# Expert routing by top-8 search with indices on two token halves, in a two-layer encoder

## The chip, the cores and the metric

One core of one Trainium2 chip runs the whole program. The metric is the device time of one execution in microseconds (us). The core has TensorE (PE; PEld is its weight load), VectorE (DVE), ScalarE (ACT), GpSimd (POOL) and SyncE (SP), each with its own queue of instructions in order; 16 DMA engines are shared by the queues that issue DMAs (here SP, ACT and POOL).

## The reference, cut to what matters

Two layers, 512 tokens of width 1024, each with a mixer, a cross-attention and a mixture of 16 experts, in which every expert picks its 64 best tokens:

```python
def expert_choice_moe(h, w_router, w_gate, w_up, w_down):   # h: (1, 512, 1024), normed x
    cap = EC_CAPACITY_FACTOR * S // N_EXPERTS                # 64
    affinity = jax.nn.softmax((h @ w_router).astype(jnp.float32), axis=-1)
    gate, idx = lax.top_k(jnp.swapaxes(affinity, 1, 2), cap)
    x_in = jax.vmap(lambda hb, ib: hb[ib])(h, idx)
    a = jnp.einsum('becd,edf->becf', x_in, w_gate)
    u = jnp.einsum('becd,edf->becf', x_in, w_up)
    y = jnp.einsum('becf,efd->becd', jax.nn.silu(a) * u, w_down)
    y = y * gate[..., None].astype(y.dtype)
    return ...                                               # y added at rows idx
```

## The kernel before, in words

The tokens stand on the 128 partitions in four blocks (b). A layer runs the mixer, the cross-attention and the experts in this order. The last stage of the cross-attention adds its output to x (out_block), transposes x (features), makes router logits (logits, scaled) and the softmax (affinity, `aff`), and turns it to 16 experts by 512 tokens (turned, into `pT`). out_block also writes the plain x of each block to `xrows` in HBM, from ScalarE's queue (L876).

**Routing (L943 to L991).** Eight rounds on VectorE take the eight largest of each expert's row (MAX8, L976) and replace them by -1 (L977). Where the row is below -0.5 the token is chosen (L981); a scan over the tokens numbers the chosen ones (L982), transposes bring mask and numbers back to tokens on partitions (L987), and `pos` holds the place of each token in each expert's list, or 0 (L991). `warm` puts idle matmuls on TensorE behind some of these steps. GpSimd meanwhile splits affinity and norm factor into high and low parts (`affs`, with the token number beside them). In layer 0 the matmuls of next_keys, for layer 1, fill TensorE at this time, and ScalarE copies their result to kT (L854).

**Experts (L993 to L1224).** They run in eight pairs, one expert's 64 tokens in each half of the array's columns. one_hot compares `pos` with the numbers 1 to 64 on VectorE. fetch multiplies the one-hots with `affs` (four matmuls, L1089), casts the token number (L1091), gathers the 128 rows from `xrows` by an indirect DMA on GpSimd's queue (L1093) and adds the two parts of gate and norm factor. features_of transposes the rows (L1072) and scales them (L1075). up_half (L1108) and down (L1127) are the expert matmuls; selection transposes the one-hots (L1081) and copies them on ScalarE (L1083), and scatter multiplies them with y and adds to x (L1141, L1142). Iteration e does pair e's gate and up projections and pair e-1's down projection and scatter; pair e+2's fetch stands at its end.

**The weights** (512 KB tiles `ew`, 192 per layer) come through a ring of buffers on SP's queue (L1028). Some lie in memory that the stage before frees (`ewb`, EW_B of them); a tile loads when its buffer's last reader is done. `lnf`, the gain of the last norm, is loaded from ScalarE's queue (L1215) into a buffer of the tag "oh".

**The order.** The program is written once, and a planner puts each engine's instructions in order at build time, from its own costs, with earlier program text first among what it believes ready. It can move work far ahead of its text, and its order holds whatever the real times are. Buffers of a tag are handed on in turn, and a DMA issue can wait for a DMA that it shares no data with, as a weight load on SP does for that of `lnf`. The lines that set the ring and the warming:

```python
        ring = [(ew, "ew", EW_KEEP)] * EW_KEEP + [(kt, "kt", 1)] * (l > 0) + [(ewa, "ew", EW_A)] * (EW_A - pre)
        once = {22: (mp, "y", 2), 23: (mp, "y", 2)}
        early = len(ring)
        ring += [(ewb, "ew", EW_B)] * EW_B + [(ewa, "ew", EW_A)] * pre
```

Of the kernel before, what the change touches and what calls it, by code (L numbers as in the profile page):

```python
# [16 lines left out]
P = 128  # L17
D = 1024
# [10 lines left out]
EW_B = 12  # L29
# [4 lines left out]
WARM_T = (1, 3)  # L34
# [23 lines left out]
def kernel(ctx: ExitStack, tc: tile.TileContext, a: dict, out: bass.AP):  # L58
# [31 lines left out]
    iota = const.tile([P, CAP], F32, name="iota")  # L90
    ids = const.tile([P, NB], F32, name="ids")
    fold = const.tile([P, NE], F32, name="fold")
    ident_r = const.tile([P, P], F32R, name="ident_r")

    def late_constants():
        nc.sync.dma_start(iota, a["iota"])
        nc.sync.dma_start(ids, a["ids"])
        nc.sync.dma_start(fold, a["fold"])
        nc.vector.tensor_copy(ident_r, ident)
# [108 lines left out]
    for l in range(L):  # L208
# [657 lines left out]
        aff = const.tile([P, NB, NE], F32, tag="aff", name=nm("aff"))  # L866
# [39 lines left out]
        def affinity(b):  # L906
# [37 lines left out]
        small = mp.tile([P, 1024], F32, tag="xg", name=nm("small"), bufs=3)  # L944
        affr = small[:, 0:2 * NB * NE].rearrange("p (b e c) -> p b e c", b=NB, e=NE)
        mkt = small[:, 256:256 + NB * NE].rearrange("p (g b e) -> p g b e", g=4, b=NB)
        m8 = small[:NE, 512:512 + CAP]

        affs = mp.tile([P, NB, NE // 2, 10], F32R, name=nm("affs"))
        pos = mp.tile([P, 4, NB, 4], F32, name=nm("pos"))  # L950
# [4 lines left out]
        parts = affs.rearrange("p b q c -> p (b q) c")[:, :, 0:8].rearrange("p q (i h c) -> p q i h c", i=2, h=2)  # L955
        whole = affr.rearrange("p b (q i) c -> p (b q) i c", i=2)
        nc.gpsimd.tensor_copy(parts[:, :, :, 0, :], whole)
        nc.gpsimd.tensor_tensor(out=parts[:, :, :, 1, :], in0=whole, in1=parts[:, :, :, 0, :].bitcast(F32),
                                op=ALU.subtract)
        for q in range(NE // 2):  # L960
            nc.gpsimd.tensor_copy(affs[:, :, q, 8:10], ids.unsqueeze(2).broadcast_to([P, NB, 2]))
        if l < L - 1:
            next_keys(range(NK0, ND))
        work = mp.tile([P, 2, S], F32, tag="oh", name=nm("work"), bufs=2)
        wk, cs = work[:NE, 0, :], work[:NE, 1, :]
# [24 lines left out]
        nc.scalar.copy(mkt, pv[0])  # L990
        nc.vector.tensor_tensor(out=pos, in0=pv[1], in1=mkt, op=ALU.mult)  # L991
# [58 lines left out]
        ohs = {}  # L1050

        def one_hot(g):

            oh = mp.tile([P, NB, 256], F32R, tag="oh", name=nm("oh"), bufs=2)
            for b0, nb in ([(b, 1) for b in range(NB)] if g == 0 else [(0, NB)]):
                nc.vector.tensor_tensor(
                    out=oh[:, b0:b0 + nb].rearrange("p b (e s) -> p (b e) s", s=CAP),
                    in0=pos[:, g, b0:b0 + nb].rearrange("p b e -> p (b e)").unsqueeze(2).broadcast_to([P, nb * 4, CAP]),
# [244 lines left out]
```

## Time and profile before

| what | us |
|---|---|
| median of 3 runs (lowest, highest) | 1205.39 (1204.15, 1206.23) |
| the profiled execution's own time | 1205.65 |
| its span, first to last instruction | 1203.9 |
| TensorE busy | 1146.7 (95%) |
| VectorE busy | 622.8 (52%) |
| ScalarE busy | 500.5 (42%) |
| GpSimd busy | 197.6 (16%) |
| TensorE's share of the chain that ended last | 82% |
| the same chain over DMAs | 7% |
| the same chain over VectorE | 6% |

Busy shares are averages over stages with different limits; the chain is followed back from the last instruction to what released each step. Matmuls overlap, so the busy time of a group of matmuls is longer than the time between the starts of two groups. In the chain a line "PE ps L1108 x16" is sixteen matmul instructions; an fp32 matmul is two.

### The profile page before, as it was taken

The numbers are of one execution on the slowest core, as the hardware profiler recorded it, in microseconds if no ns is written. First come the engines' busy times: TensorE is split into PE (matmuls) and PEld (weight loads), VectorE is DVE, ScalarE is ACT, GpSimd is POOL, SyncE is SP. The second block draws the span as 40 slices with busy tenths as digits, with TensorE's granted clock in tenths as the row PEclk, the third lists the DMA queues.
The fourth block names the chain that finished last, engine by engine and source line by source line (L and its number), as shares of the span: only waits on it lengthen the run. The fifth ranks groups of instructions, "written<-read, shape, count | busy, mean of one in ns | idle before, by whom it ended". The sixth has DMA issues, their size and how long they took to land.

```text
span 1203.9 us, 16694 instructions
## 1 busy us (share of the span) xinstructions
PE 1146.7 (95%) x5992; PEld 741.2 (62%) x5992; DVE 622.8 (52%) x1405; ACT 500.5 (42%) x1140; POOL 197.6 (16%) x258
## 2 busy tenths in 40 slices
PE   7999999999997999999999999999998699999995
PEld 7977777887673444333389677778876334443332
DVE  4898877555561222222278888775465503332224
ACT  5388757464422121111154887674454021211103
POOL 2633413100011000000035333230001000000002
PEclk9999999999998999999999999999999799999998
DMA  6310011375078999999344100117813599997994
GB/s 192 129 66 19 19 36 36 123 286 221 19 286 330 415 410 416 414 411 416 156 123 132 52 19 18 36 53 261 298 35 137 214 391 416 411 414 306 349 416 179
DMA packets 78930, 260.50 MB, mean 216 GB/s; under 512 B 8704, under 2 KB 18816, under 8 KB 78848
## 3 DMA queue, kind: packets, MB, share of 16 engines
q1 hardware_dynamic: 74960, 246.23, 53.2%
q0 software_dynamic: 2304, 8.39, 1.9%
q10 hardware_dynamic: 1584, 4.83, 1.1%
q8 instruction: 47, 0.77, 0.3%
q14 instruction: 35, 0.29, 0.1%
HBM read 253.12 MB, written 6.29 MB: 215 GB/s over the span
## 4 chain that ended last, share of the span: by engine, by line
PE 82%; DMA 7%; DVE 6%; ACT 2%; issue 1%; POOL 0%; SPq 0%; POOLq 0%; DVEq 0%; ACTq 0%
PE ps L1108 17%; PE ps L147 11%; PE ps L148 10%; PE ps L149 10%; PE ps L1127 8%; PE ps L1141 5%; PE ps L410 5%; DMA ew<-moe 4%; PE ps L396 4%; DMA rows<-xrows,row 2%; PE ps L1072 2%; DVE smm L184 2%; PE ps L491 2%; PE ps L807 1%; PE ps L253 1%
## 5 line engine op out<-in xcount | busy, mean ns | idle before, releaser
L1108 PE MATMUL ps<-ew,xg 128*64 128x512 f32 x1024 | 256.6, 604 | 0.3 <-DMA ew<-moe 0.3
L1108 PEld LDWEIGHTS ps<-ew,xg 128*64 128x64 f32 x1024 | 74.6, 138 | 138.4 <-issue 121.6
L117 DVE TENSOR_TENSOR y<-ps,y 128x512 fp32r<-128x512 f32 x32 | 22.1, 692 | 216.3 <-ACT y L116 216.3
L1127 PE MATMUL ps<-ew,hT 128*64 128x512 f32 x512 | 118.5, 594 | 0.2 <-DMA ew<-moe 0.2
L117 DVE TENSOR_TENSOR wlo<-raw,whi 128x1024 fp32r<-128x1024 f32 (+2 forms) x72 | 82.0, 1143 | 56.5 <-ACT whi L116 50.5
L184 DVE TENSOR_REDUCE smm<-ps 128x1 f32<-128x512 f32 (+1 forms) x144 | 97.6, 681 | 18.2 <-PE ps L491 7.6
L190 ACT ACTIVATE P<-ps,smm 128x512 f32<-128x512 f32 x128 | 88.8, 696 | 27.8 <-DVE smm L184 22.0
L1142 DVE TENSOR_TENSOR x<-ps,x 128x512 f32<-128x512 f32 x128 | 80.7, 684 | 38.0 <-PE ps L1141 37.5
L116 ACT CAST whi<-raw 128x1024 fp32r<-128x1024 f32 (+2 forms) x72 | 70.0, 973 | 65.8 <-PE ps L148 35.9
L199 POOL TENSOR_TENSOR P<-P,smr 128x512 f32<-128x512 f32 x64 | 70.3, 1098 | 155.9 <-DVE smr L197 129.0
L116 ACT CAST y<-ps 128x512 fp32r<-128x512 f32 x32 | 18.7, 585 | 157.0 <-PE ps L1127 154.2
L1127 PEld LDWEIGHTS ps<-ew,hT 128*64 128x64 f32 x512 | 38.0, 137 | 72.9 <-issue 70.0
L396 PE MATMUL ps<-ident,P 128*128 128x128 f32 x512 | 76.9, 274 | 2.9 <-POOL P L199 0.9
L147 PE MATMUL ps<-whi,hTh 128*128 128x384 f32 (+2 forms) x224 | 79.2, 353 | 0.2 <-ACT whi L116 0.2
L148 PE MATMUL ps<-whi,hTl 128*128 128x384 f32 (+2 forms) x224 | 78.4, 350 | 0.0
L149 PE MATMUL ps<-wlo,hTh 128*128 128x384 f32 (+2 forms) x224 | 77.9, 350 | 0.0
L396 PEld LDWEIGHTS ps<-ident,P 128*128 128x128 f32 x512 | 62.6, 141 | 22.8 <-issue 4.2
L1141 PE MATMUL ps<-y,sel 128*128 128x512 f32 x256 | 70.3, 411 | 1.5 <-ACT y L116 1.5
L1093 POOL DMA_INDIRECT rows<-xrows,row x16 | 15.4, 962 | 332.0 <-DVE g L1099 296.5
L399 ACT COPY PT<-ps 128x512 f32<-128x512 f32 x96 | 56.0, 588 | 24.5 <-PE ps L396 24.0
L1141 PEld LDWEIGHTS ps<-y,sel 128*128 128x128 f32 x256 | 45.4, 188 | 31.6 <-issue 17.0
L1075 ACT ACTIVATE xg<-ps,gains 128x128 f32<-128x128 f32 x128 | 36.3, 372 | 67.7 <-PE ps L1072 67.7
(223 smaller groups left out, 2124.5 us busy)
## 6 DMA issues: line engine op xcount, KB each, us to landing
ew<-moe SPq DMA_DIRECT2D x384, 512.0 KB, 10.2
raw<-w_o SPq DMA_DIRECT2D x16, 512.0 KB, 3.8
raw<-w_mem_v SPq DMA_DIRECT2D x8, 512.0 KB, 3.4
raw<-w_mem_q SPq DMA_DIRECT2D x8, 512.0 KB, 4.5
raw<-w_mem_o SPq DMA_DIRECT2D x8, 512.0 KB, 4.1
xrows<-x ACTq DMA_DIRECT2D x8, 512.0 KB, 2.6
raw<-w_in_c SPq DMA_DIRECT2D x8, 416.0 KB, 3.6
raw<-w_in_a SPq DMA_DIRECT2D x8, 384.0 KB, 4.7
```

Source lines behind the costliest of these rows:

```text
L116: i = nc.scalar.copy(dst_hi, src)
L117: nc.vector.tensor_tensor(out=dst_lo, in0=src, in1=dst_hi.bitcast(F32), op=ALU.subtract)
L147: nc.tensor.matmul(o, lh, rh, start=start, stop=False)
L148: nc.tensor.matmul(o, ll, rh, start=False, stop=False)
L149: nc.tensor.matmul(o, lh, rl, start=False, stop=stop)
L184: nc.vector.tensor_reduce(out=m, in_=s.rearrange("p (g n) -> p g n", g=groups), axis=AX.X, op=ALU.max, negate=True)
L190: nc.scalar.activation(p[:, g * n:(g + 1) * n], s[:, g * n:(g + 1) * n], AF.Exp, bias=m[:, g:g + 1], scale=1.0 if scale is None else scale ...
L396: nc.tensor.transpose(pt[:, tb * P:(tb + 1) * P], u.p[:, tb * P:(tb + 1) * P], ident)
L1108: nc.tensor.matmul(acc[i * 64:i * 64 + 64, :], e.xg[:, k, i * 64:i * 64 + 64], ch[i][j % 2], start=k == 0, stop=k == 7)
L1127: nc.tensor.matmul(e.py[i * 64:i * 64 + 64, :], e.hT[:, f, i * 64:i * 64 + 64], ch[i][j], start=f == 0, stop=f == 3)
L1141: nc.tensor.matmul(o, sl, e.y[n][i], start=i == 0, stop=i == 1)
L1142: nc.vector.tensor_tensor(out=x[:, b, ns], in0=o, in1=x[:, b, ns], op=ALU.add)
```

## The change

Affinities are padded to 32 columns and turned so that an expert's first 256 tokens stand on one partition and its last 256 on another, 32 further on. Each round is MAX8, an index search (max_index) and a replace over 256 columns. The two sorted lists of 64 are merged by comparing the first with the reverse of the second: at each place the larger value and its token. Four small matmuls put token and gate of each pair in a column; `row`, `tok` and `gate` serve all pairs. The selection is a comparison of the token numbers 0 to 511 with `tok` on VectorE. `xrows` now holds the normed x, which ScalarE makes (rows_out) after the affinities, in halves of 256 KB; the norm factor leaves silu. Fourteen warming matmuls stand behind the first two fetches, half of the first pair's feature scaling goes to VectorE, the ring has one buffer more, `iota` is 256 KB, and `lnf` takes a buffer of the tag "rows".

```diff
-EW_B = 12
+EW_B = 13
 WARM = 3
-WARM_T = (1, 3)
+WARM_F = 14
...
-        aff = const.tile([P, NB, NE], F32, tag="aff", name=nm("aff"))
+        aff = const.tile([P, NB, 32], F32, tag="aff", name=nm("aff"))
+        nc.gpsimd.memset(aff[:, :, NE:32], 0.0)
...
             if n == 1:
-                nc.scalar.dma_start(xrows[b * P:(b + 1) * P, :], x[:, b, :])
                 ffn_norm.rstd(b)
...
         def turned(b):
             if b == 0:
                 plg["T"] = bank()
-            nc.tensor.transpose(plg["T"][:NE, b * P:(b + 1) * P], aff[:, b, :], ident)
+            h, c = 32 * (b // 2), b % 2 * P
+            nc.tensor.matmul(plg["T"][h:h + 32, c:c + P], aff[:, b, :], ident, start=True, stop=True)
+
+        def rows_out(b):
+
+            for n in range(2):
+                t = cp.tile([P, 512], F32, tag="P", name=nm("xn"), bufs=P_BUFS)
+                ns = slice(n * 512, n * 512 + 512)
+                nc.scalar.activation(t, x[:, b, ns], AF.Copy, scale=ffn_norm.r[:, b:b + 1])
+                nc.scalar.dma_start(xrows[b * P:(b + 1) * P, ns], t)
...
         turned(NB - 1)
+        for b in range(NB):
+            rows_out(b)
         pT = plg["T"]
...
+        tk = mp.tile([64, 1024], F32, tag="xg", name=nm("tk"), bufs=3)
+        wk, m8 = tk[:, 0:256], tk[:, 256:256 + CAP]
+        at8 = mp.tile([64, CAP], mybir.dt.uint32, name=nm("at8"))
+        tok = mp.tile([P, NE // 2], F32, name=nm("tok"))
+        gate = mp.tile([P, NE // 2], F32, name=nm("gate"))
+        row = mp.tile([P, NE // 2], mybir.dt.int32, name=nm("row"))
         ewb = moe.enter_context(tc.tile_pool(name=f"ewb{l}", bufs=EW_B, reuse_waits="tile"))
-        rsb = ffn_norm.r.unsqueeze(2).broadcast_to([P, NB, NE])
-        nc.gpsimd.tensor_tensor(out=affr[:, :, :, 0], in0=aff, in1=rsb, op=ALU.mult)
-        nc.gpsimd.tensor_copy(affr[:, :, :, 1], rsb)
...
         def warm(behind, n):
 
-            nc.tensor.matmul(idle[:8, 0:P], behind, ident[:NE, :], start=True, stop=True)
+            if behind is not None:
+                nc.tensor.matmul(idle[:8, 0:P], behind, ident[:64, :], start=True, stop=True)
             for _ in range(n):
                 nc.tensor.matmul(idle[:, 0:256], x[:, 0, 0:P], x[:, 0, 0:256], start=True, stop=True)
 
+
         for i in range(CAP // 8):
-            src = wk if i else pT[:NE, :]
-            nc.vector.max(out=m8[:, 8 * i:8 * i + 8], in_=src)
-            nc.vector.match_replace(out=wk, in_to_replace=m8[:, 8 * i:8 * i + 8], in_values=src, imm_value=-1.0)
+            src, best = wk if i else pT[0:64, 0:256], m8[:, 8 * i:8 * i + 8]
+            nc.vector.max(out=best, in_=src)
+            nc.vector.max_index(out=at8[:, 8 * i:8 * i + 8], in_max=best, in_values=src)
+            if i < CAP // 8 - 1:
+                nc.vector.match_replace(out=wk, in_to_replace=best, in_values=src, imm_value=-1.0)
             if i >= WARM_FROM[l]:
-                warm(m8[:, 8 * i:8 * i + 8], WARM)
-        mk = wk
-        nc.vector.tensor_scalar(mk, wk, -0.5, None, op0=ALU.is_le)
-        nc.vector.tensor_tensor_scan(out=cs, data0=ones[:NE, :].broadcast_to([NE, S]), data1=mk, initial=0.0,
-                                     op0=ALU.mult, op1=ALU.add)
-        pp = [bank() for _ in range(2)]
-        for t, src in zip(pp, (mk, cs)):
-            for b in range(NB):
-                nc.tensor.transpose(t[:, b * NE:(b + 1) * NE], src[:, b * P:(b + 1) * P], ident[:NE, :NE])
-            warm(src[:, 0:8], WARM_T[src is cs])
-        pv = [t[:, 0:NB * NE].rearrange("p (b g e) -> p g b e", g=4, e=4) for t in pp]
-        nc.scalar.copy(mkt, pv[0])
-        nc.vector.tensor_tensor(out=pos, in0=pv[1], in1=mkt, op=ALU.mult)
+                warm(best, WARM)
+
+        c = [tk[0:NE, 320 + CAP * i:320 + CAP * i + CAP] for i in range(5)]
+        m2, t1, t2, dt, later = c
+        nc.scalar.copy(m2, m8[32:32 + NE, ::-1])
+        nc.vector.tensor_copy(t1, at8[0:NE, :])
+        nc.vector.tensor_scalar(t2, at8[32:32 + NE, ::-1], float(S // 2), None, op0=ALU.add)
+        nc.vector.tensor_tensor(out=later, in0=m2, in1=m8[0:NE, :], op=ALU.is_gt)
+        nc.vector.tensor_tensor(out=dt, in0=t2, in1=t1, op=ALU.subtract)
+        nc.vector.tensor_tensor(out=dt, in0=dt, in1=later, op=ALU.mult)
+        nc.vector.tensor_tensor(out=t1, in0=t1, in1=dt, op=ALU.add)
+        nc.vector.tensor_tensor(out=m2, in0=m2, in1=m8[0:NE, :], op=ALU.max)
+
+        pk = bank()
+        for j, src in enumerate((t1, m2)):
+            for i in range(2):
+                nc.tensor.matmul(pk[i * 64:i * 64 + 64, j * 8:j * 8 + 8], src, ident[0:NE, i:NE:2], start=True, stop=True)
+        nc.vector.tensor_copy(row, pk[:, 0:8])
+        nc.scalar.copy(tok, pk[:, 0:8])
+        nc.scalar.copy(gate, pk[:, 8:16])
...
+        for p, e in enumerate(prs):
+            e.p = p
...
-                nc.scalar.activation(e.xg[:, d, :], pt[:, i * P:(i + 1) * P], AF.Copy, scale=gain(l, G_FFN, d))
+                if e.p == 0 and i % 2:
+                    nc.vector.tensor_scalar(e.xg[:, d, :], pt[:, i * P:(i + 1) * P], gain(l, G_FFN, d), None, op0=ALU.mult)
+                else:
+                    nc.scalar.activation(e.xg[:, d, :], pt[:, i * P:(i + 1) * P], AF.Copy, scale=gain(l, G_FFN, d))
 
         def selection(e):
-            pS = bank()
-            pSr = pS.bitcast(F32R)
-            for b in range(NB):
-                nc.tensor.transpose(pSr[:, b * P:(b + 1) * P], e.oh[:, b, :], ident_r)
-            e.sel = mp.tile([P, S], F32R, tag="sel", name=nm("sel"), bufs=1)
-            nc.scalar.copy(e.sel, pS)
+
+            e.sel = mp.tile([P, S], F32R, tag="sel", name=nm("sel"), bufs=2)
+            nc.vector.tensor_scalar(e.sel, iota, tok[:, e.p:e.p + 1], None, op0=ALU.is_equal)
...
         def fetch(e):
 
-            pgt = bank()
-            for b in range(NB):
-                nc.tensor.matmul(pgt[:, 0:10], e.oh[:, b, :], affs[:, b, e.p, :], start=b == 0, stop=b == NB - 1)
...
             e.rows = mp.tile([P, D], F32, tag="rows", name=nm("rows"), bufs=2)
             nc.gpsimd.indirect_dma_start(out=e.rows, out_offset=None, in_=xrows,
-                                         in_offset=bass.IndirectOffsetOnAxis(ap=at_row, axis=0))
-            e.gt = mp.tile([P, 2], F32, tag="gt", name=nm("gt"), bufs=4)
...
+                                         in_offset=bass.IndirectOffsetOnAxis(ap=row[:, e.p:e.p + 1], axis=0))
...
-        one_hot(0)
         for e in prs[:2]:
             fetch(e)
+        warm(None, WARM_F)
         for n in range(2):
             features_of(prs[0], n)
...
-            nc.scalar.activation(sg, ag, AF.Silu, scale=e.gt[:, 1:2])
-            nc.vector.scalar_tensor_tensor(out=sg, in0=au, scalar=e.gt[:, 0:1], in1=sg, op0=ALU.mult, op1=ALU.mult)
+            nc.scalar.activation(sg, ag, AF.Silu)
+            nc.vector.scalar_tensor_tensor(out=sg, in0=au, scalar=gate[:, e.p:e.p + 1], in1=sg, op0=ALU.mult,
+                                           op1=ALU.mult)
             e.hid = sg
...
-            lnf = mp.tile([P, D], F32, tag="oh", name=nm("lnf"), bufs=2)
+            lnf = mp.tile([P, D], F32, tag="rows", name=nm("lnf"), bufs=2)
             nc.scalar.dma_start(lnf, a["lnf"])
...
-    a["iota"] = np.ascontiguousarray(np.broadcast_to(np.arange(1, CAP + 1, dtype=np.float32)[None], (P, CAP)))
-    a["ids"] = np.ascontiguousarray(np.arange(S, dtype=np.float32).reshape(NB, P).T)
+    a["iota"] = np.ascontiguousarray(np.broadcast_to(np.arange(S, dtype=np.float32)[None], (P, S)))
```

## Rows read from the trace of the kernel before

**Rows 1.** Chain of waits in order of time, layer 0's experts: start us, us, what.
```profile
363.21 7.56 DMA rows<-xrows,row
...
372.84 4.75 PE ps L1108 x16
...
406.71 3.43 PE ps L1108 x16
...
453.84 6.87 PE ps L1127 x32
...
480.83 6.87 PE ps L1127 x32
...
504.44 1.86 PE ps L1108 x6
...
511.86 6.87 PE ps L1127 x32
```

**Rows 2.** Stretches of layer 1: us, busy us by engine, granted clock, DMA share, GB/s.
```profile
944.00:956.00 12.00, 7.43 (x42) 5.27 (x42) 5.05 (x17) 0.21 (x1) 2.02 (x2) 0.98 0.32 111
956.00:968.00 12.00, 10.95 (x44) 4.62 (x46) 0.00 (x0) 4.59 (x13) 0.00 (x0) 0.74 0.54 187
...
1088.00:1100.00 12.00, 12.00 (x55) 4.17 (x53) 0.00 (x0) 1.72 (x5) 0.00 (x0) 1.00 1.03 415
1100.00:1112.00 12.00, 12.00 (x49) 4.61 (x46) 3.97 (x10) 2.79 (x7) 0.94 (x1) 1.00 0.54 197
```

**Rows 3.** What SP's queue waited for: us in total, times, longest us.
```profile
SPq L1028 <- DMA lnf<-lnf: 19.5, 1, 19.5
```

**Rows 4.** The chain of waits in order of time, layer 1's experts.
```profile
952.59 4.32 DMA rows<-xrows,row
...
958.99 5.22 PE ps L1108 x16
...
1122.28 11.95 DMA ew<-moe
```

**Rows 5.** Timeline, layer 1's search: start us, us, what, idle time before it.
```profile
931.62 0.69 DVE L976 MAX8 small<-ps 16x8 f32<-16x512 f32 x1 [0.37 <-PE ps L921]
...
933.12 0.68 DVE L976 MAX8 small<-work 16x8 f32<-16x512 f32 x1
...
933.84 0.08 DVE L977 MATCH_VALUE_LOAD work<-small,work 16x8 f32 x1
933.91 0.67 DVE L977 MATCH_REPLACE8 work<-small,work 16x512 f32<-16x512 f32 x1
```

**Rows 6.** Timeline, layer 1: end of its routing, and a part of its first pair.
```profile
949.08 1.56 PE L972 MATMUL ps<-x 128*128 128x256 f32 x6
...
952.59 1.08 POOL L1093 DMA_INDIRECT rows<-xrows,row  x1 [18.87 <-DVE gt L1100]
...
972.16 0.59 PE L1089 MATMUL ps<-affs,oh 128*128 128x10 f32 x4
...
972.60 0.53 PE L1081 MATMUL ps<-ident_r,oh 128*128 128x128 f32 x4
...
973.06 7.09 PE L1108 MATMUL ps<-ew,xg 128*64 128x512 f32 x32
```

**Rows 7.** Timeline, layer 0's search and ScalarE beside its end.
```profile
345.15 0.69 DVE L976 MAX8 small<-ps 16x8 f32<-16x512 f32 x1 [0.37 <-PE ps L921]
...
355.52 1.67 ACT L854 COPY kT<-ps 128x256 f32<-128x256 f32 x4 [11.20 <-PE ps L850]
```

**Rows 8.** Groups of VectorE by shape: busy us, mean ns, idle before.
```profile
L891 DVE COPY rht<-ps 128x256 f32<-128x256 f32 x16 | 6.8, 422 | 1.4 <-ACT rht L890 0.5
...
L991 DVE TENSOR_TENSOR pos<-ps,small 128x64 f32<-128x64 f32 x2 | 0.4, 224 | 4.4 <-PE ps L987 4.4
```

**Rows 9.** Timeline, layer 0: the third pair's rows come in.
```profile
395.61 0.66 PE L1072 MATMUL ps<-ident,rows 128*128 128x128 f32 x4 [1.49 <-DMA rows<-xrows,row]
```

**Rows 10.** ScalarE's scaled copy of 128x512, group by shape.
```profile
L1160 ACT ACTIVATE ew<-ew,nr 128x512 f32<-128x512 f32 x4 | 2.9, 718 | 1.4 <-POOL nr L172 1.3
```

More of the change, by code (lines that the diff above doesn't have):

```diff
@@ L89 @@
     nc.gpsimd.memset(ones, 1.0)
-    iota = const.tile([P, CAP], F32, name="iota")
-    ids = const.tile([P, NB], F32, name="ids")
+    iota = const.tile([P, S], F32, name="iota")
     fold = const.tile([P, NE], F32, name="fold")
-    ident_r = const.tile([P, P], F32R, name="ident_r")
     def late_constants():
         nc.sync.dma_start(iota, a["iota"])
-        nc.sync.dma_start(ids, a["ids"])
         nc.sync.dma_start(fold, a["fold"])
-        nc.vector.tensor_copy(ident_r, ident)
     G_MIX, G_MEM, G_MKV, G_FFN, G_CQ, G_CKV, G_OG, G_OM = 0, 8, 16, 24, 32, 34, 35, 39
@@ L943 @@
         mp = moe.enter_context(tc.tile_pool(name=f"moe{l}", bufs=1, reuse_waits="tile"))
[L944 to L950, printed above, removed]
-        ewb = moe.enter_context(tc.tile_pool(name=f"ewb{l}", bufs=EW_B, reuse_waits="tile"))
-        rsb = ffn_norm.r.unsqueeze(2).broadcast_to([P, NB, NE])
-        nc.gpsimd.tensor_tensor(out=affr[:, :, :, 0], in0=aff, in1=rsb, op=ALU.mult)
-        nc.gpsimd.tensor_copy(affr[:, :, :, 1], rsb)
[L955 to L961, printed above, removed]
+        tk = mp.tile([64, 1024], F32, tag="xg", name=nm("tk"), bufs=3)
[4 more added lines that the diff above has]
+        row = mp.tile([P, NE // 2], mybir.dt.int32, name=nm("row"))
+        ewb = moe.enter_context(tc.tile_pool(name=f"ewb{l}", bufs=EW_B, reuse_waits="tile"))
         if l < L - 1:
             next_keys(range(NK0, ND))
-        work = mp.tile([P, 2, S], F32, tag="oh", name=nm("work"), bufs=2)
-        wk, cs = work[:NE, 0, :], work[:NE, 1, :]
         idle = bank()
         def warm(behind, n):
-            nc.tensor.matmul(idle[:8, 0:P], behind, ident[:NE, :], start=True, stop=True)
+            if behind is not None:
+                nc.tensor.matmul(idle[:8, 0:P], behind, ident[:64, :], start=True, stop=True)
             for _ in range(n):
@@ L1049 @@
         prs = [Experts() for _ in range(NE // 2)]
[L1050 to L1058, printed above, removed]
-                    in1=iota.unsqueeze(1).broadcast_to([P, nb * 4, CAP]), op=ALU.is_equal)
-            for i in range(2):
-                e = prs[2 * g + i]
-                e.p = 2 * g + i
-                e.oh = oh[:, :, i * P:i * P + P]
+        for p, e in enumerate(prs):
+            e.p = p
         def features_of(e, n):
@@ L1074, in features_of @@
                 d = n * 4 + i
-                nc.scalar.activation(e.xg[:, d, :], pt[:, i * P:(i + 1) * P], AF.Copy, scale=gain(l, G_FFN, d))
+                if e.p == 0 and i % 2:
+                    nc.vector.tensor_scalar(e.xg[:, d, :], pt[:, i * P:(i + 1) * P], gain(l, G_FFN, d), None, op0=ALU.mult)
+                else:
+                    nc.scalar.activation(e.xg[:, d, :], pt[:, i * P:(i + 1) * P], AF.Copy, scale=gain(l, G_FFN, d))
         def selection(e):
-            pS = bank()
-            pSr = pS.bitcast(F32R)
-            for b in range(NB):
-                nc.tensor.transpose(pSr[:, b * P:(b + 1) * P], e.oh[:, b, :], ident_r)
-            e.sel = mp.tile([P, S], F32R, tag="sel", name=nm("sel"), bufs=1)
-            nc.scalar.copy(e.sel, pS)
-        def fetch(e):
-            pgt = bank()
-            for b in range(NB):
-                nc.tensor.matmul(pgt[:, 0:10], e.oh[:, b, :], affs[:, b, e.p, :], start=b == 0, stop=b == NB - 1)
-            at_row = mp.tile([P, 1], mybir.dt.int32, tag="row", name=nm("row"), bufs=4)
-            nc.vector.tensor_copy(at_row, pgt[:, 8:9])
+            e.sel = mp.tile([P, S], F32R, tag="sel", name=nm("sel"), bufs=2)
+            nc.vector.tensor_scalar(e.sel, iota, tok[:, e.p:e.p + 1], None, op0=ALU.is_equal)
+        def fetch(e):
             e.rows = mp.tile([P, D], F32, tag="rows", name=nm("rows"), bufs=2)
             nc.gpsimd.indirect_dma_start(out=e.rows, out_offset=None, in_=xrows,
-                                         in_offset=bass.IndirectOffsetOnAxis(ap=at_row, axis=0))
-            e.gt = mp.tile([P, 2], F32, tag="gt", name=nm("gt"), bufs=4)
-            g2 = mp.tile([P, 2], F32, tag="g2", name=nm("g2"), bufs=2)
-            for i in range(2):
-                sl = slice(i * 64, i * 64 + 64)
-                nc.vector.tensor_copy(g2[sl, :], pgt[sl, 4 * i:4 * i + 2])
-                nc.vector.tensor_tensor(out=e.gt[sl, :], in0=pgt[sl, 4 * i + 2:4 * i + 4], in1=g2[sl, :], op=ALU.add)
+                                         in_offset=bass.IndirectOffsetOnAxis(ap=row[:, e.p:e.p + 1], axis=0))
         def up_half(e, acc, w, kc):
@@ L1177 @@
             end = e.p == NE // 2 - 1
-            if e.p % 2 == 0 and not end and e.p + 2 < NE // 2:
-                one_hot(e.p // 2 + 1)
             ag = bank()
```

4 lines of the change are left out of this document (2 added, 2 removed).

## The prediction

> **What bounds the kernel now.** I read first the page's 40 slices and its chain by engine: TensorE is busy nearly throughout and carries most of the chain, so a change that shortens VectorE's work counts only where TensorE waits for it. Then the chain in order of time, for two stretches in each layer: the routing head, between the last router logits and the first expert matmul, and the expert pairs.
>
> In the pairs the chain is TensorE after TensorE. The down projections of successive pairs start 480.83 - 453.84 = 27.0 us apart while the order is whole, and 511.86 - 480.83 = 31.0 us apart later [rows 1]. Nothing waits for weights in that 31.0: the planner has cut the matmul blocks there and put scatter pieces between. Six L1108 matmuls alone take 1.86 us, where sixteen together take 3.43, so 1.29 for six: 0.57 per break [rows 1].
>
> The weight stream is the second bound. At 415 GB/s a 524 KB tile takes 1.26 us, and a pair needs 24 tiles and a row fetch, about 31.6 us, more than a whole-order pair of TensorE. In layer 1 the stream stands partly idle while its buffers are full (DMA share 0.32 and 0.54 of a full 1.03: 8.3 and 5.7 us lost) and again at 1100 (0.54) [rows 2], where SP's queue waits 19.5 us for the load of lnf [rows 3]. Behind that the chain goes over weight tiles [rows 4]. So layer 0 is TensorE's; in layer 1's second half both bounds lie close together.
>
> **Search.** Before, from the first maximum to the first row fetch: 952.59 - 931.62 = 20.97 us in layer 1 [rows 5, 6]; 363.21 - 345.15 = 18.06 us in layer 0 [rows 1, 7]. A round is a maximum (0.68), a value load (0.08) and a replace (0.67) with 0.06 of gaps, 1.49 us, eight times [rows 5]. After, each works on 256 columns: from the groups of 256 and 64 columns one column is (422 - 224)/192 = 1.03 ns [rows 8], so 256 fewer save 0.26: 0.42 and 0.41. The trace has no index search; I price it as a load and a replace of that length (0.49 + 0.03), its nearest row. A round is 1.49 and the last, without replace, 0.97: 7 x 1.49 + 0.97 = 11.4 us against 11.9. Bounds: a free search gives 7.3; all three at full length 17.4 (a round of 2.27).
>
> The Trainium skill (Vector Engine (DVE) Microarchitecture Reference, 3.9) says that the maximum leaves no positions and that finding them is a separate value load and a streaming pass. No run here shows it; by it the free end falls away, and the sum stays.
>
> **Merge.** Removed behind the search: compare, scan, eight transposes, pos, one-hots, eight gather matmuls. Added: seven small VectorE operations at 0.22 (the 128x64 group [rows 8]) = 1.5 us, four fp32 matmuls in eight passes, two of the blocks of four that take 0.44 (972.60 - 972.16 [rows 6]) = 0.9, a cast and hand-offs, 0.5. From the first maximum to the fetch: 11.4 + 2.9 = 14.3 us. In layer 0 the reversed copy stands on ScalarE behind the kT copies, which end at 357.19, 1.3 us behind the last maximum as I place it (345.15 + 7 x 1.49 + 0.42 = 356.0) [rows 7]; VectorE has its index search and two other operations meanwhile, so I add 0.5: 14.8. Saved: 3.3 us in layer 0, 6.7 in layer 1 (the small operations at half or double: 0.8 less, 1.5 more per layer).
>
> **Rows and warming.** The first rows landed in 7.56 us in layer 0, where the stream was running [rows 1], and in 4.32 in layer 1, where it stood mostly idle [rows 2, 4]. The row writes (2 MB, 5 us of stream) now come after the norm, and one more weight tile is loaded, so layer 1's fetch falls into traffic: I take 7.0, nearer to the row with the stream running, +2.7 (bounds 0 to 3.2). The 14 warming matmuls take 14 x 1.56/3 = 7.3 us [rows 6] and fit in that landing; with rows at 4.3 they would be the last to end, so the 2.7 stands either way. They stand behind the merge's matmuls in the program, and a planner that sets them ahead costs at most that much. The granted clock was 0.74 of full in 956 to 968 [rows 2], a mixture of the levels of 1.2 and 2.4 GHz, and the first sixteen matmuls took 4.75 and 5.22 us against 3.43 [rows 1, 4]: 1.3 and 1.8 to win, 0 to lose. I take 1.0 each, since the planner may spread the warming.
>
> **Pairs.** The gather matmuls and the selection transposes hold TensorE from 972.16 to 973.06: 0.44 and 0.46 [rows 6]. Six gathers (the first two are in the head) and eight selections per layer: 2.6 + 3.7 = 6.3 us, all on the chain. What replaces them, a 128x512 compare, goes to VectorE, which waits for TensorE there; ScalarE loses its copy of the selection. With VectorE's cover gone each would cost at most a 512-column operation per pair, 0.68 by the maximum's row [rows 5]. The fetches no longer wait for TensorE: the third pair's wait of 1.49 in layer 0 [rows 9] goes. After it the next late thing is the weight stream.
>
> **What is moved.** The eight scaled copies ahead of the writes are new on ScalarE, 0.72 each [rows 10]; their issues stand on ScalarE's queue, and the later ones wait for one of five P buffers, with the affinity's exp, the merge's copy and xg behind them. I take +0.6 per layer, one copy pushed ahead of an exp (0 to two copies, 1.4). The fetch on POOL's queue now also waits for these writes; they have 14 us, and if they are late the price is one landing, up to 7.56. New weight tiles that lie over P buffers make SP's queue wait for those writes, the whole stream behind it; the idle 8.3 + 5.7 us of layer 1 [rows 2] cover that, less what the earlier start uses up. The table of 256 KB costs 0.5 us of stream at the start, beside projections: 0 (up to 0.5).
>
> **The planner's order.** Faster pairs use up the loaded tiles sooner, so the cut order may begin a pair earlier. One more cut pair costs 31.0 - 27.0 = 4.0 us [rows 1]; I take half, +2.0 per layer (from -11, no cuts, to +16, all pairs cut).
>
> **Sum.** Layer 0: -3.3 - 1.0 - 6.3 - 1.5 + 0.6 + 2.0 = -9.5. Layer 1: -6.7 + 2.7 - 1.0 - 6.3 + 0.6 + 2.0 = -8.7. The stream must allow the latter: its free run starts with the first freed buffer, 4 to 5 us earlier, one buffer more is 1.3, and the wait for lnf should shrink, since lnf now takes a rows buffer that is free earlier; I count 3 of the roughly 6 us lost in 1100 to 1112 [rows 2]. That is 8.7 too. The profiled execution took 1205.65 us (span 1203.9); less 18.2 is 1187.4. It stands 0.26 above the median of the runs, so I predict 1187.
>
> **The rivals.**
> *The stream takes layer 1's gain.* If the lnf wait stays and SP waits for the row writes, layer 1 gains 4 rather than 8.7: 1192, and up to 1200 where layer 0's stream is held too. For it: the tiles on the chain behind 1122 [rows 4]; against it: the idle 14 us.
> *The halved search is no shorter.* If operations on 64 partitions take what 512 columns take, each layer loses 6.0: 1199. For it: the halves stand on 64 partitions where 16 were, and no row shows these operations so; against it: the column slope [rows 8].
> *Slower: the order breaks up.* If the planner, with the lead used up sooner, cuts the four whole pairs of each layer as well, that is 4 x 4.0 - 2.0 = 14 more per layer, 28 in all: 1215. It decides from about 2.8 pairs per layer, where 9.1 + 2.0 are eaten. For it: the 4.0 was paid with no weight wait to justify it [rows 1]; against it: one buffer more, and about 1 us less work per pair moves the onset by less than a pair. The Trainium skill (TensorEngine Tiling (Array Packing), Key Properties) says that a change of tiling mode drains TensorE; by that rule each such cut costs, and the trace agrees with 0.57 per break [rows 1].
> *Better: the cuts vanish.* With the selection no longer on TensorE and one more buffer: 13 less in layer 0, up to 5 in layer 1: 1169 to 1174.
>
> **How the numbers follow.** My forecast 0.52 (own range 1180 to 1195), stream 0.18, search 0.07, better 0.08, order 0.11, and 0.04 for a cancelling in between. A measurement of this kernel tells about 0.2% (2.4 us) from no change. Faster 0.85, same 0.04, slower 0.11. The range leaves out the better case's far end and the order's: 1173 to 1203.
>
> **What would show it.** Right: the fetch 14 to 15 us behind the first maximum, index searches of about 0.4 us, whole pairs at 26 us, the first sixteen expert matmuls near 3.4 us, no wait for rows in the third pair. Wrong: searches of 0.67; down projections 30 us apart from the first pairs on; idle DMA with SP waiting for xrows or lnf; or a fetch whose last releaser is a row write.

## The result, and the profile after

The changed kernel takes 1185.39 us (median of 4 runs, 1183.77 to 1187.64), the kernel before 1204.77 beside it: a ratio of 0.9839 [0.9819, 0.9859]. Predicted were 1187 and a range of 1173 to 1203. A second set of runs (changed_again) gave 1185.28 and 0.9831 [0.9818, 0.9845]. The profiled execution took 1184.8 us, with this span; the chain that ended last goes over TensorE for 85% (82% before), over VectorE for 5% and over DMAs for 4% (6% and 7% before):

```profile
span 1183.0 us, 16485 instructions
...
PE 85%; DVE 5%; DMA 4%; ACT 3%; issue 2%; POOL 0%; SPq 0%; ACTq 0%; POOLq 0%; DVEq 0%
```

**Search and merge.** The timeline of VectorE in layer 1, from the first maximum on (start us, us, what):

```profile
920.71 0.42 DVE L972 MAX8 tk<-ps 64x8 f32<-64x256 f32 x1 [0.50 <-PE ps L918]
...
922.53 0.08 DVE L973 MATCH_VALUE_LOAD at<-tk 64x8 f32 x1
922.61 0.41 DVE L973 FIND_INDEX8 at<-tk 64x8 uint32<-64x256 f32 x1
923.05 0.08 DVE L975 MATCH_VALUE_LOAD tk<-tk 64x8 f32 x1
923.13 0.40 DVE L975 MATCH_REPLACE8 tk<-tk 64x256 f32<-64x256 f32 x1
923.57 0.42 DVE L972 MAX8 tk<-tk 64x8 f32<-64x256 f32 x1
...
933.04 0.21 DVE L987 TENSOR_TENSOR tk<-tk 16x64 f32<-16x64 f32 x1
```

A round is 923.57 - 922.08 = 1.49 us, as predicted and as long as a round before, which had no index search [rows 5]. Each index search takes a value load of 0.08 and a pass of 0.41. The Trainium skill (Vector Engine (DVE) Microarchitecture Reference, 3.9) says that finding the positions is a value load and a pass of its own; the trace agrees. VectorE ends the merge at 933.25. TensorE's timeline there, from the first warming group of the last four rounds on (a group is two small matmuls, L965, and six on x, L967):

```profile
927.02 0.59 PE L965 MATMUL ps<-ident,tk 64*8 64x128 f32 x2 [6.35 <-DVE tk L972]
927.54 2.93 PE L967 MATMUL ps<-x 128*128 128x256 f32 x6
...
930.92 1.56 PE L967 MATMUL ps<-x 128*128 128x256 f32 x6
...
932.73 1.56 PE L967 MATMUL ps<-x 128*128 128x256 f32 x6
...
934.53 1.56 PE L967 MATMUL ps<-x 128*128 128x256 f32 x6
936.02 0.40 PE L993 MATMUL ps<-ident,tk 16*64 16x8 f32 x8
936.35 6.31 PE L967 MATMUL ps<-x 128*128 128x256 f32 x28
944.69 1.09 PE L1065 MATMUL ps<-ident,rows 128*128 128x128 f32 x8 [2.03 <-DMA rows<-xrows,row]
```

The merge's own matmuls (L993) begin at 936.02, 2.77 us after their data, behind warming groups queued ahead of them. In layer 0, which has no such groups, VectorE's timeline shows the first maximum and the first operation of the merge:

```profile
346.81 0.42 DVE L972 MAX8 tk<-ps 64x8 f32<-64x256 f32 x1 [1.18 <-PE ps L918]
...
358.47 0.21 DVE L984 TENSOR_TENSOR tk<-tk 16x64 f32<-16x64 f32 x1 [0.40 <-ACT tk L981]
```

The fetch starts 936.92 - 920.71 = 16.21 us after the first maximum in layer 1 and 360.83 - 346.81 = 14.02 in layer 0, against 20.97 and 18.06 [rows 1, 5 to 7].

**Rows and pairs.** The chain of waits, layer 0's experts and the head of layer 1's (L1065 transposes the rows, L1090 and L1109 are the expert matmuls):

```profile
360.83 7.50 DMA rows<-xrows,row
368.47 1.06 PE ps L1065 x8
369.56 3.65 PE ps L1090 x16
...
419.21 6.87 PE ps L1109 x32
...
445.39 6.87 PE ps L1109 x32
...
501.81 6.87 PE ps L1109 x32
...
532.06 6.87 PE ps L1109 x32
...
936.92 7.72 DMA rows<-xrows,row
...
945.80 3.65 PE ps L1090 x16
```

The first sixteen expert matmuls take 3.65 us in both layers (4.75 and 5.22 [rows 1, 4]); down projections of whole pairs stand 445.39 - 419.21 = 26.2 us apart, of pairs that the planner has cut 532.06 - 501.81 = 30.25 (27.0 and 31.0 [rows 1]). As many pairs are whole as before, four a layer. The rows land in 7.72 us in layer 1, where they had 4.32 [rows 4].

**The stream.** Stretches of layer 1 (busy us by engine, granted clock, DMA share, GB/s), and SP's wait for lnf:

```profile
944.00:956.00 12.00, 11.29 (x56) 4.40 (x58) 1.40 (x4) 4.48 (x10) 0.93 (x1) 1.00 0.86 315
956.00:968.00 12.00, 12.00 (x62) 4.54 (x60) 0.75 (x1) 2.78 (x9) 0.94 (x1) 1.00 1.02 411
...
1076.00:1088.00 12.00, 12.00 (x55) 4.16 (x52) 2.08 (x3) 2.81 (x7) 0.00 (x0) 1.00 0.70 271
1088.00:1100.00 12.00, 11.91 (x43) 4.54 (x42) 5.61 (x9) 0.00 (x0) 0.00 (x0) 1.00 0.85 328
```

```profile
SPq L1033 <- DMA lnf<-lnf: 12.2, 1, 12.2
```

The first pair's stretch, from 944 here and from 956 before, has a granted clock of 1.00 where it was 0.74; between 944 and 968 the DMA share is 0.86 and 1.02 where it was 0.32 and 0.54 [rows 2]. The wait for lnf is 12.2 us, was 19.5 [rows 3]; at 1076 to 1100 the stream still loses (1.03 - 0.70 + 1.03 - 0.85) x 12 / 1.03 = 5.9 us.

By stage, from the two traces (us saved are negative):

| stage | predicted, layer 0 / 1 | measured, layer 0 / 1 |
|---|---|---|
| moved work: last out_block to first maximum | +0.6 / +0.6 | +1.5 / +0.1 |
| first maximum to fetch | -3.3 / -6.7 | -4.0 / -4.8 |
| landing of the rows | 0 / +2.7 | -0.1 / +3.4 |
| clock: first transposes and sixteen matmuls | -1.0 / -1.0 | -1.9 / -2.5 |
| rest of the experts | -7.8 / -6.3 | -6.9 / -6.2 |
| planner's order | +2.0 / +2.0 | 0 (in the row above) |
| sum | -9.5 / -8.7 | -11.4 / -10.0 |

The measured sums and +0.5 at the start, between the layers and in the tail make up the 20.9 us between the spans. The table is of one execution each; the clock's row differs between executions (below, under the warming).

### The profile page after: what moved, and what is told of

Same layout as the page of the kernel before. It is cut to its first block, busy times and chain, and to the rows that moved or that the text cites. A ratio compares the mean times of both kernels' runs of the same rounds, so it can differ in the third digit from the quotient of the medians.

```text
span 1183.0 us, 16485 instructions
## 1 busy us (share of the span) xinstructions
PE 1139.2 (96%) x5904; PEld 731.3 (62%) x5904; DVE 609.6 (52%) x1372; ACT 499.3 (42%) x1136; POOL 193.6 (16%) x236
## 4 chain that ended last, share of the span: by engine, by line
PE 85%; DVE 5%; DMA 4%; ACT 3%; issue 2%; POOL 0%; SPq 0%; ACTq 0%; POOLq 0%; DVEq 0%
PE ps L1090 19%; PE ps L143 11%; PE ps L144 10%; PE ps L145 10%; PE ps L1109 10%; PE ps L1123 5%; PE ps L406 5%; PE ps L392 4%; DVE smm L180 2%; PE ps L487 2%; PE ps L1065 1%; DMA ew<-moe 1%; DMA rows<-xrows,row 1%; PE ps L803 1%; PE ps L249 1%
## 5 line engine op out<-in xcount | busy, mean ns | idle before, releaser
L1090 PE MATMUL ps<-ew,xg 128*64 128x512 f32 x1024 | 253.9, 598 | 0.0
L1090 PEld LDWEIGHTS ps<-ew,xg 128*64 128x64 f32 x1024 | 74.0, 136 | 140.2 <-issue 131.5
L1109 PE MATMUL ps<-ew,hT 128*64 128x512 f32 x512 | 116.9, 593 | 0.0
L1099 ACT COPY hT<-ps 128x512 f32<-128x512 f32 x16 | 9.4, 586 | 174.0 <-PE ps L1096 174.0
L1109 PEld LDWEIGHTS ps<-ew,hT 128*64 128x64 f32 x512 | 37.3, 137 | 73.0 <-issue 70.9
L168 POOL TENSOR_TENSOR nr<-nv,mhalf 128x1 f32<-128x1 f32 x32 | 18.9, 595 | 244.4 <-DVE nv L167 224.4
```

The costliest lines, as they stand in the source:

```text
L1090: nc.tensor.matmul(acc[i * 64:i * 64 + 64, :], e.xg[:, k, i * 64:i * 64 + 64], ch[i][j % 2], start=k == 0, stop=k == 7)
L1109: nc.tensor.matmul(e.py[i * 64:i * 64 + 64, :], e.hT[:, f, i * 64:i * 64 + 64], ch[i][j], start=f == 0, stop=f == 3)
```

## The experiments

Ratios are to the kernel before, run beside; the changed kernel's own two ratios differ by 0.0008.

**The search by itself (search_doubled).** Is the price per operation the one on the path?

```diff
+            for _ in range(2):
                 nc.vector.max_index(out=at8[:, 8 * i:8 * i + 8], in_max=best, in_values=src)
```

> The changed kernel with every index search done twice. Theory A, the routing head is on the path one to one: 8 more searches of 0.52 us in each layer; 4.1 us in layer 0, about the same in layer 1, 7 to 9 us slower in all, about 1193. Theory B, the start of the experts is set by the weight stream or by the row writes: under 3 us slower.

1189.22 us, 0.9857 [0.9841, 0.9874]: 3.8 more than the changed kernel, where 7 to 9 were expected. In layer 0 the fetch came 17.8 us after the first maximum: +3.8, about eight times 0.41 + 0.08, and nothing of it was given back. In layer 1 the fetch came only 2.4 later, since the merge's matmuls stood behind the warming groups for 1.05 us instead of 2.77. That 2.4 was given back too: the rows landed in 6.17 us instead of 7.72, and one cut pair, in which the planner's order had fewer breaks, took 29.0 instead of 30.2. From the last out_block to the end of the last scatter layer 1 took 260.5 us, 260.7 in the changed kernel. So the search is on the path at its own length in layer 0; in layer 1 this run shows no cost of it.

**The matmuls removed from the pairs (matmuls_put_back).** refill is four matmuls of 128x128 (fp32r) and four of 10 columns, in place of the selection's and the gather's; its results are used nowhere.

```diff
                 selection(e)
+                refill(e)
```

> The changed kernel with, in each of the first seven pairs of a layer, four 128x128 matmuls and four of ten columns put on TensorE behind the selection, of the shapes that the change took away; their results are used by nothing. Theory A, what the pairs gained was this work: 0.8 to 0.9 us per pair and 14 pairs, 11 to 13 us slower, about 1197. Theory B, the pairs are set by the weight stream and the gain came from the routing head: under 4 us slower.

1193.56 us, 0.9902 [0.9882, 0.9921]: 8.2 more than the changed kernel, where 11 to 13 were expected. Its chain, layer 0:

```profile
420.97 6.87 PE ps L1117 x32
...
447.95 6.87 PE ps L1117 x32
...
505.96 6.87 PE ps L1117 x32
...
537.01 6.87 PE ps L1117 x32
```

Whole pairs are 27.0 us again and cut ones 31.0, to the tenth [rows 1], and layer 0's experts take 5.6 us more. Layer 1's took only 1.5 more, because there the planner left one pair more whole, worth 4.0. So the pairs' term was what was removed from TensorE.

**The warming (no_warming).** `WARM_F = 0`: the matmuls behind the fetch are left out.

> The changed kernel without the fourteen warming matmuls between fetch and features. Theory A, the clock falls while TensorE waits for the rows: the eight transposes take 1.9 instead of 1.1 us and the first sixteen expert matmuls 4.7 to 5.2 instead of 3.65, 3.5 to 5 us slower in all, about 1189. Theory B, the warming changes the start only and the stream gives it back: under 1 us. Theory C, the warming delays more than it wins: faster.

1190.45 us, 0.9864 [0.9848, 0.9881]: 5.1 more. Stretches and chain of layer 0 without them:

```profile
360.00:372.00 12.00, 2.46 (x18) 2.07 (x20) 2.61 (x11) 0.76 (x4) 2.14 (x2) 0.60 1.03 420
372.00:384.00 12.00, 12.00 (x48) 3.83 (x48) 0.96 (x3) 3.86 (x9) 0.93 (x1) 0.83 1.03 420
```

```profile
369.94 1.94 PE ps L1065 x8
371.88 5.72 PE ps L1090 x16
```

With TensorE busy 2.46 of 12 us the granted clock is 0.60, a mixture of the 1.2 and 2.4 GHz levels, and the transposes and sixteen matmuls take 7.7 us instead of 4.7. From the fetch to the last scatter layer 0 is 3.2 us longer and layer 1 1.5; the rest of the 5.1 lies ahead of layer 0's routing, where nothing was changed.

The warming does not hold the clock in every execution, though. changed_again is the same kernel, and its trace has this in layer 0 (TensorE's timeline):

```profile
369.39 1.94 PE L1065 MATMUL ps<-ident,rows 128*128 128x128 f32 x8 [2.15 <-DMA rows<-xrows,row]
371.26 4.38 PE L1090 MATMUL ps<-ew,xg 128*64 128x512 f32 x16
```

The fourteen warming matmuls had run at the upper level throughout, in 6.31 us, and ended 2.15 us before the transposes; from 369.4 to 373.4 the granted clock was 0.58. In the first trace they had begun at a lower clock, taken 8.00 us and ended 0.23 before the transposes, and the clock stayed at 1.00. So in changed_again 1.5 of the 1.9 us won in layer 0 are lost again.

**Layer 1's queue at the merge (warm_earlier, warm_gap).** warm_earlier ends layer 1's warming groups after the sixth of eight rounds; warm_gap also puts 22 matmuls instead of 14 behind the fetch.

```diff
-WARM_FROM = (8, 4)
+WARM_FROM = (8, 3)
+WARM_TO = 6
...
-            if i >= WARM_FROM[l]:
+            if WARM_FROM[l] <= i < WARM_TO:
```

> The changed kernel with layer 1's warming groups behind rounds 3 to 5 of the search instead of 4 to 7. Theory A, the merge's matmuls stand 2.8 us in TensorE's queue behind the last warming groups (ready at 933.25, begun at 936.02 in the changed kernel's trace) and the expert stage starts as much later: 2 to 2.8 us faster, about 1183, with 13.5 to 14.2 us from layer 1's first maximum to its first row fetch (16.2 now). Theory B, layer 1 is set by the weight stream, not by its start: no change, although the fetch comes earlier. Theory C, the clock falls without the late groups: the first sixteen expert matmuls take over 4.5 us again and the gain is lost.

> As warm_earlier (the warming groups of layer 1 end after the sixth round of eight), with 22 instead of 14 matmuls behind the row fetch of layer 1, so that TensorE works until about 1 us before the rows land instead of 2.8. Theory C (in warm_earlier the granted clock fell in the first pair because TensorE stood still): the fetch is again 13.8 us after the first maximum, the first sixteen expert matmuls of layer 1 take 3.65 us and not 5.35, the experts' stage is 226.0 and not 227.7, and the layer is 2.0 to 2.5 us shorter than in the changed kernel: 1182.5 to 1183.5. Rival A (the stream gives the end of layer 1, an earlier start is waited off later): experts 228, time as changed_again, 1184.5 to 1186. Rival D (the rows land later with more work on TensorE): fetch to first transposes over 8.5 us.

warm_earlier: 1184.95 us, 0.9826 [0.9813, 0.984], no gain, though the fetch came 13.7 us after the first maximum instead of 16.2. warm_gap: 1183.58, 0.9812 [0.9798, 0.9825]. The stretch in which the first pair begins, in warm_earlier and then in warm_gap:

```profile
944.00:948.00 4.00, 4.00 (x12) 1.10 (x10) 1.09 (x4) 0.80 (x3) 0.89 (x1) 0.59 0.88 320
```

```profile
944.00:948.00 4.00, 3.98 (x20) 1.26 (x19) 1.40 (x4) 1.26 (x4) 0.94 (x1) 1.00 0.96 349
```

In warm_earlier TensorE had stood still for 2.81 us before the first transposes, and the granted clock was 0.59 in the next stretch; the first sixteen matmuls took 5.35 us. In the changed kernel it had stood for 2.03 and the clock stayed at 1.00. In warm_gap it did not stand still, the clock stayed at 1.00 too, and they took 3.65. Of the 2.5 us that warm_earlier won in the queue, the clock took 1.7 and a landing of 8.08 us 0.4. By its median warm_gap is 1.7 us ahead of changed_again, but the intervals overlap, and 1.2 of what its trace gains in layer 1 is a cut pair of 29.0 in which the planner's order had fewer breaks.

**Layer 0's later search (keys_behind).** In the changed kernel the search of layer 0 begins 9.4 us after the last out_block, 1.5 later than before. TensorE's timeline there:

```profile
341.95 0.41 PE L894 MATMUL ps<-rht,wrg 128*32 128x128 f32 x4
342.29 1.13 PE L846 MATMUL ps<-ew,ew 128*128 128x256 f32 x4
...
343.69 0.40 PE L900 MATMUL ps<-fold,lgt 128*128 128x16 f32 x2
343.93 1.11 PE L846 MATMUL ps<-ew,ew 128*128 128x256 f32 x4
344.97 0.41 PE L918 MATMUL ps<-ident,aff 128*32 128x128 f32 x2
345.31 1.13 PE L846 MATMUL ps<-ew,ew 128*128 128x256 f32 x4
346.37 0.41 PE L918 MATMUL ps<-ident,aff 128*32 128x128 f32 x2
```

next_keys (L846) stands between the router's matmuls (L894, L900) and the turns (L918). The edit forces it behind the last of the turns:

```diff
+            with tc.issue_after(plg["last"].ins):
+                next_keys(range(NK0))
```

> The first layer's 64 key-projection matmuls (the line that multiplies memory features by w_mem_k of layer 1) are all forced behind the last transpose of the affinities; nothing else changes by hand. What it tells: why the search of layer 0 begins 9.4 us after the last out_block in the changed kernel and not 7.8 as before. Theory K (the key matmuls that stand between the affinity matmuls in TensorE's queue): the search begins 7.4 to 8.2 us after the last out_block, 1.2 to 2 us earlier; but the keys then end 2 to 3 us later and the merge's small matmuls stand behind them, so that the row fetch comes no earlier than in the changed kernel, up to 2 us later, and the whole is 0 to 3 us longer. Rival X, the prediction's own step (an xn copy ahead of an exp on ScalarE): the search still begins 9.0 us or more after the last out_block.

1190.38 us, 0.9867 [0.9852, 0.9882]: 5.0 more, where 0 to 3 were expected. The search began 7.2 us after the last out_block, 2.2 earlier: the key matmuls were the cause, not a scaled copy on ScalarE, as the prediction had it. But they now end at 360.3, and the fetch, counted from the last out_block, comes 2.5 us later than in the changed kernel. ScalarE copies them to kT, and the merge's reversed copy stands behind; VectorE waits for it:

```profile
355.48 0.41 DVE L974 FIND_INDEX8 at<-tk 64x8 uint32<-64x256 f32 x1
361.00 0.21 DVE L985 TENSOR_TENSOR tk<-tk 16x64 f32<-16x64 f32 x1 [5.11 <-ACT tk L982]
```

This is the wait that the prediction priced at 0.5 us, and that is 0.40 in the changed kernel's order. The clock took 1.6 more: TensorE stood still for 2.04 us before the first transposes, and the first sixteen matmuls took 5.28 us. The tiles of w_mem_k that they read give their buffers to the weight stream, whose share at 350 to 360 fell to 0.71 (1.00 in the changed kernel). The planner's place for the keys is the better one.

**The order and the stream (whole_order, lnf_own_buffer, one_buffer_less, whole_lnf).** whole_order ties each block of a pair's matmuls behind the last matmul of the block before, so that no pair is cut (one call is shown; hid_t, features_of, down and scatter go the same way):

```diff
+        def behind(f, *args):
+            with tc.issue_after(mm[0].ins) if mm[0] is not None else ExitStack():
+                f(*args)
...
-            up_half(e, ag, 0, 0)
+            behind(up_half, e, ag, 0, 0)
```

> The changed kernel with TensorE's order in the pairs held to the order of the text up to the seventh pair, so that no scatter pieces and features stand inside matmul blocks. Theory A, each cut pair costs 4.0 us for nothing: three pairs in each layer go from 30.2 to 26.2 us, 24 us faster, about 1161. Theory B, the weight stream lies close behind: in the changed kernel the last tiles land about 6 us before their use in both layers, so TensorE waits for tiles instead and at most some 12 us can be gained, 1173 to 1180, with visible waits for weight tiles. Theory C, the cuts only fill waits that would be there anyway: no change.

1182.12 us, 0.9793 [0.9777, 0.9809]: only 3.2 less than changed_again, where three cut pairs a layer at 4.0 each would have made 24, and the theory of tiles close behind had 1173 to 1180. The chain in layer 0 says why:

```profile
471.46 6.84 PE ps L1116 x31
478.30 11.38 DMA ew<-moe
...
499.99 9.88 DMA ew<-moe
...
530.13 10.18 DMA ew<-moe
```

From 478 on it goes over weight tiles, and the last starts of silu, one a pair, are 30.2 us apart, 24 tiles of 1.26. Layer 0's experts gain 0.5 us. SP issues layer 0's last tile at 574.6 before, 575.2 in the changed kernel and 575.6 here, while the last scatter matmul began at 606.8, 595.5 and 594.9: the stream has not moved, and TensorE has come up to it, from 32.2 us behind the last tile to 20.3 and 19.3.

one_buffer_less sets EW_B to 12; lnf_own_buffer does so too and loads `lnf` early into a tile of its own; whole_lnf is whole_order with that tile and 13 buffers.

```diff
         last_norm = x_norm()
+        if l == L - 1:
+            lnf = mp.tile([P, D], F32, name=nm("lnf"))
+            nc.scalar.dma_start(lnf, a["lnf"])
```

> The changed kernel with 12 weight buffers of the second kind, as before the change, instead of 13. Theory A, TensorE's order is the bound and the tiles come early enough: no change (within 1 us). Theory B, the weight stream is the bound in layer 1's second half: 1.3 us slower per layer, 1 to 3 in all.

> As the run with 12 buffers, and lnf in a buffer of its own, loaded early in layer 1, so that SP's queue does not wait 12.2 us for it. Theory A, TensorE's order is the bound: the idle stretch of the DMA engines at 1076 to 1100 goes, and the time stays within 1 us of the run with 12 buffers. Theory B, the stream is the bound there: 3 to 5 us faster than that run.

> The order of whole_order with the last norm's gains in a tile of their own, loaded when the layer's expert stage begins, so that SP's weight stream no longer waits for them; thirteen buffers as before. Theory S (with every pair whole, the end of the experts is set by the stream, and the stream lost about 3.5 us in layer 1 from 1090 to 1120, where the transfers' share was 0.91 instead of 1.03): layer 1's experts 220 instead of 223.4, time 1178.0 to 1180.0. Rival A (TensorE sets the end of layer 1 also there): 1181.5 to 1183. Rival B (the extra transfer early, 512 KB, takes the stream 1.3 us): up to 1184.

one_buffer_less: 1184.78 us, 0.983 [0.9816, 0.9843], no change. lnf_own_buffer: 1187.86, 0.9844 [0.9828, 0.9859], no gain, although SP no longer waited and the share at 1076 to 1100 was 1.03. The planner's new order also put the fetch of layer 1 1.6 us later, and TensorE, still for 2.32 us, began the first pair at a clock of 0.60 (the first sixteen matmuls took 5.11). Behind these, to the end of the last scatter, layer 1 took 224.7 us, as in the changed kernel: the freed stream itself gave nothing. whole_lnf: 1177.09, 0.9758 [0.9745, 0.9772], 5.0 below whole_order. Its stretches of layer 1:

```profile
1060.00:1090.00 30.00, 30.00 (x144) 14.08 (x144) 10.20 (x17) 5.58 (x16) 0.94 (x1) 1.00 1.03 412
1090.00:1120.00 30.00, 30.00 (x144) 12.14 (x144) 9.88 (x17) 4.44 (x12) 0.00 (x0) 1.00 1.03 414
```

Six of layer 1's periods between silus are 26.2 us or less and the seventh 27.8 (30.2, 30.3 and 29.5 for the last three in the changed kernel), and its experts take 216.8 us instead of 226.0. Either edit alone leaves the other's bound standing: whole pairs wait for a stream that stood still for lnf, and a stream that does not stand still feeds cut pairs, which went on taking 30.2 in lnf_own_buffer.

**All of it (whole_lnf_warm).** whole_lnf and warm_gap together.

> whole_lnf and warm_gap together: every pair whole, the last norm's gains in their own tile, layer 1's warming groups ended after the sixth round and 22 matmuls behind its row fetch. Theory: the two gains add, since a layer that starts earlier frees its buffers earlier and the stream with them; whole_lnf was 1177.1, its layer 1 began its experts 1.3 us later than the changed kernel's (first maximum to first expert matmul 26.7 against 25.1), and warm_gap had 23.5: 3 us earlier, 1173.5 to 1175. Rival (the stream alone sets the end of layer 1 and does not start earlier): 1176.5 to 1178, with the last weight tile issued at 1144 as in whole_lnf.

1172.85 us (1171.73 to 1173.51), 0.9719 [0.9706, 0.9732]: the fastest of the runs, and below the 1173.5 to 1175 expected. Layer 1's fetch comes 14.9 us after the first maximum (16.9 in whole_lnf), and the first transposes and sixteen matmuls are 1.3 us shorter, because whole_lnf had lost its clock there (TensorE still for 2.63 us) and this run did not. SP issues the last tile at 1140.8 instead of 1144.4, so the stream did move with the start, and layer 0's experts take 224.9 in both: layer 0 is at its stream.

## Why the prediction was right

- **Search.** Right: 11.3 us to the end of the last index search, of which a round is 1.49; the priced-by-neighbour index search (0.49 with its load) measured 0.49.
- **Merge.** Layer 0's 14.8 was 14.0: the reversed copy on ScalarE held VectorE for 0.40 us, where 0.5 was added (the 1.3 beside it is 357.19 - 356.0 = 1.2), and the rest of the merge took 2.4 instead of 2.9. Layer 1's 14.3 was 16.2. The step that failed is the one that costed the warming groups at nothing there: the prediction had the 14 matmuls behind the merge in mind, and overlooked the groups of the last four rounds, queued one a round. The first of them runs at half the clock (0.50 from 927 to 930.4) and takes 2.93 us instead of 1.56, so that the second begins 1.9 us behind its round; the others begin 1.81 us apart, at 930.92, 932.73 and 934.53, against 1.49 a round, and add 0.3 to 0.5 each. The merge's matmuls stand behind the last of them. warm_earlier and warm_gap, 2.5 and 2.3 us earlier there, show that the groups are the cause.
- **Rows.** The landing of 7.7 us in traffic was forecast at 7.0, from 4.3. No run took the traffic away, so that it is the traffic is argued from the shares and not shown: 1.02 during the landing, 0.59 in the 4.32 us before, the rows included, and 0.95 in search_doubled, where it took 6.17.
- **Warming.** The term was mis-sized: 1.9 and 2.5, not 1.0, because the transposes (1.94 to 1.06) run at the higher clock too. no_warming shows the size, 3.2 and 1.5. That it came whole in the measured kernel's trace is in part luck: fourteen matmuls were priced at 7.3 us, take 6.31 at the full clock, and leave about 2 us in which TensorE stands still. In layer 1 the clock outlasted that in both traces of the kernel, in layer 0 it did not in changed_again.
- **Pairs.** Right in mechanism and size: 0.81 a whole pair and 0.78 a cut one of the 0.90 summed from two gaps; matmuls_put_back gives back exactly 27.0 and 31.0. The third pair's wait for its rows is gone, as forecast.
- **Moved work.** +0.6 per layer came as +1.5 and +0.1, by another cause: the key matmuls in TensorE's queue (keys_behind).
- **The planner's order.** +2.0 per layer did not come; the cut begins at the same pair. What stood behind it was wrong as well: "One more cut pair costs 31.0 - 27.0 = 4.0 us" and "Nothing waits for weights in that 31.0" read an idle-free TensorE as the only bound. In whole_order the whole pairs wait for tiles and take 30.2. The prediction had the 24 tiles of 1.26 us in the paragraph below, and did not put them beside the 31.0. The breaks of 0.57 are there, and under the stream's pace they cost 0.5 us in all of layer 0. So its "better" rival, 1169 to 1174 for vanished cuts, was priced wrongly: whole order alone gave 1182.
- **The stream in layer 1.** It did not take the gain, and that it moved was a condition. Before, the last tile of layer 1 was issued at 1173.3 and the last scatter matmul began 19.4 us later; 19.2 to 19.5 is the distance wherever whole order brought TensorE up to the stream (whole_order, whole_lnf, whole_lnf_warm, both layers). With the tiles on its chain [rows 4], layer 1 thus ended at its stream before the change. In the changed kernel the last tile comes 11.7 us earlier, counted from the last out_block, and the distance is 21.2. More than that gave nothing: one_buffer_less is as fast without the thirteenth buffer counted at 1.3, and freeing the stream of lnf entirely gains nothing while pairs are cut (lnf_own_buffer). How much of the gain the old wait of 19.5 us would have taken, no run shows.

The forecast of -18.2 us against -20.9 is thus a sum of errors of both signs, so that the total lies closer than its terms partly by luck. Measured less predicted, over both layers: moved work +0.4, merge +1.2, landing +0.6, pairs and third fetch +1.0, the clock -2.4, the order that did not break up -4.0, and +0.5 elsewhere.

## What to carry to other kernels

Where two bounds are close, price a gap of one by the pace of the other before calling it a loss: a cut order and a halting stream each looked like several us here, and only both edits together gave them. The distance from the stream's last tile to the stage's last work told here which bound held, also where TensorE showed almost no idle time. Idle work that keeps the clock up must be shorter per step than what it waits behind, its first step at the low clock included, and must reach up to the next real work: too much in the queue cost 2.8 us, too little 1.3 to 1.7. Two traces of one kernel can differ there.

## What the runs showed of the hardware

- On 64 partitions by 256 columns a MAX8 takes 0.42 us, a FIND_INDEX8 0.41 with a value load of 0.08, a replace 0.40; on 16 by 512 a maximum took 0.68 [rows 5]. Half the columns took 0.26 less, and four times the partitions added nothing that shows.
- After TensorE had stood still before the first transposes, the granted clock stayed at 1.00 where it had stood for 1.60, 1.63, 1.86, 2.03 and 2.28 us (layer 1 of matmuls_put_back, one_buffer_less, changed_again, the changed kernel and keys_behind). It fell, to 0.57 to 0.66 over the next 4 us, after 2.04 and 2.15 (layer 0 of keys_behind and changed_again) and after 2.17, 2.32, 2.63 and 2.81 (layer 1 of whole_order, lnf_own_buffer, whole_lnf and warm_earlier). These shares are mixtures of the 1.2 and 2.4 GHz levels. Between 2.04 and 2.28 us the traces show both.
- A gather of 128 rows of 4 KB landed in 7.3 to 8.1 us in most runs, with the weight stream at full share, in 6.2 in layer 1 of search_doubled at a share of 0.95, and in 4.3 in layer 1 of the kernel before at 0.59.
